# One order for every step of the attention stage: the transposes first, the projection matmuls in one run, VectorE's other work behind the maximum

## The chip, the cores and the metric

The kernel runs on one core of one Trainium2 chip. The metric is the time of one execution in device microseconds; shorter is better. TensorE is written PE, VectorE DVE, ScalarE ACT, GpSimd POOL, and SP is the queue that issues most transfers.

## What is computed

One encoder layer over 512 tokens of width 2048, in float32. An input projection gives queries, keys, values and gates for two groups of 16 heads; the group A heads use a dilated attention over all 512 keys with a bias table, the group B heads a neighbourhood attention on an 8 x 64 grid. Gated outputs go through an output projection and a layer norm.

```python
def reference(x, w_in, w_out, t5_bias, na_rpb, ln_gain, ln_bias):
    for layer in range(DEPTH):
        h = jnp.einsum('bsd,de->bse', x, w_in[layer])
        qa, ka, va, ga, qb, kb, vb, gb = jnp.split(h, splits, axis=-1)
        ya = _dilated_attention(heads(qa, N_HEADS_A), heads(ka, N_HEADS_A), heads(va, N_HEADS_A), t5_bias)
        yb = _neighbourhood_attention(heads(qb, N_HEADS_B), heads(kb, N_HEADS_B), heads(vb, N_HEADS_B), na_rpb[layer])
        ya = merge(ya) * jax.nn.silu(ga.astype(jnp.float32))
        yb = merge(yb) * jax.nn.silu(gb.astype(jnp.float32))
        out = jnp.einsum('bse,ed->bsd', jnp.concatenate([ya, yb], axis=-1), w_out[layer])
        x = _layer_norm(DEEPNORM_ALPHA * x + out, ln_gain[layer], ln_bias[layer])
    return x
```

## The kernel before

Every float32 operand of a large product is split into a high and a low part (two float32r tiles), and a product is three matmuls. Six gate columns come first, then six blocks of the input projection (queries, keys, values of both groups) by a Strassen scheme, then the attention stage (about 549 to 876 us of the profiled execution), then the rest of the output projection with the layer norm.

**The attention stage** is the loop `for n in range(136)` (L715). Step n takes one block of 128 queries of one head: head n // 4, block b = n % 4. Heads come in pairs of one group, A A B B A A ..., so a pair lasts 8 steps. The pieces of a step are:

- the scores (`scores`, L555): two matmuls into a PSUM bank `sc`, 512 columns wide in group A, 192 or 256 in group B; then on DVE the addition of the bias and the row extreme in one instruction (L525, called the maximum here), which frees the bank;
- the exponential (`exponent`, L529) on ACT;
- the turn of block n - 2 (`turn`, L581): four transposes in group A, two in group B, into a PSUM bank `pt`; then ACT copies the high part `th` (L593), and DVE subtracts it for the low part `tl` (L594), which frees the bank. `th` and `tl` of a head's four blocks lie in one tile each, "s0" and "s1", and there is one of each, so a new head's first `th` and `tl` must wait until the head before has been used;
- in the mixing steps (n % 4 == 2, from 6 to 130) the values of the head before (`values`, L599): eight matmuls into a bank of the same pool as the scores, first four that read `th`, then four that read `tl`; then ACT copies one half of the bank (`tmp`, L735), and DVE adds the other (`y`, L736), which frees the bank;
- the fillers: matmuls of the remaining gate columns (L464, while n is below about 63) and of the first half of the output projection (L658, after that), taken one at a time by `fill`. A step takes 8, 10, 8 or 1 of them up to n = 63, then 7, 8, 7 or 1 (1 in a mixing step).

Each filler weight is loaded, copied high on ACT (`wh`, L449) one step later and subtracted on DVE (`wl`, L450) two steps after its load was prepared, by a list of tasks per step (`later`), which `close` runs at the step's end. Other such tasks on DVE: the gate products (L633, L641, L643), the reciprocal of the denominators (L747), the gate's second half (L470), and the eviction of odd output banks (L664). After the fillers of each step with n % 8 == 1, `share` (L616) turns the pair's reciprocals into the other kind of row: one transpose into a bank of the turn's pool (two banks), a copy on ACT (L623), two transfers on POOL.

PE, ACT, DVE and SP run the stage in the order in which the code states it (`manual_schedule`, L708); POOL's order is the planner's. Semaphores follow from the tiles and banks.

Of the kernel before, what the change touches and what calls it, by code (L numbers as in the profile page):

```python
# [9 lines left out]
AF = mybir.ActivationFunctionType  # L10
ALU = mybir.AluOpType
# [59 lines left out]
def hybrid_layer(tc, xT, xn, w_in, w_early, w_gate, w_out, t5x, brow, rpb, cmask, eye, gain, lbias, out):  # L71
    nc = tc.nc
    from contextlib import ExitStack
    with ExitStack() as ctx:
# [8 lines left out]
        def f(ap):  # L83
            return ap.bitcast(F32)
# [9 lines left out]
        def slot(tag, dtype=F32, name=None):  # L94
            return arena.tile([128, sizes[tag[0]]], dtype, name=name or tag, tag=tag)

        class Ring:
# [3 lines left out]
            def next(self, name, dtype=F32):  # L101
                tag = self.tags[self.n % len(self.tags)]
                self.n += 1
                return slot(tag, dtype, name)

        def bank(pool, name):
            tag = {id(pacc): "acc", id(pss): "sc", id(pst): "pt"}[id(pool)]
            return pool.tile([128, 512], F32, name=name, tag=tag)
# [321 lines left out]
        step, tasks = [-PROLOGUE], {}  # L430
# [3 lines left out]
        def later(k, fn, dve=False):  # L434


            tasks.setdefault(step[0] + k, []).append((fn, dve))

        def prepare():

            while stream and len(raws) < 4:
                raws.append(raw_ring.next("wraw"))
                nc.sync.dma_start(raws[-1], stream.pop(0))
            if not raws:
                return
            raw = raws.pop(0)
            h, l = halves.next("wh", F32R), halves.next("wl", F32R)
            ready.append((h, l))
            later(1, lambda: nc.scalar.activation(h, raw, AF.Copy))  # L449
            later(2, lambda: nc.vector.tensor_tensor(l, raw, f(h), ALU.subtract), True)  # L450
# [59 lines left out]
        def load_sg(i):  # L510
            sgs[i] = sg_ring.next("sg")
            nc.sync.dma_start(sgs[i], sg_d[i])

        def softmax(sc, bias, n, grp, i, col, to=0, p=None):

            s = s_ring.next("s")
            p = p_ring.next("p") if p is None else p
            mn = small.tile([128, 1], F32, name="mn", tag="mn")
            if col == 0:
                dens[i] = small.tile([128, 8], F32, name="den", tag="den")  # L520
            den = dens[i][:, col:col + 1]
            flat = (s[:, :n], sc[:, :n])
            if grp == 1:
                flat = (t.rearrange("p (r c) -> p r c", r=8) for t in flat)
            nc.vector.tensor_tensor_reduce(*flat, bias, 1.0, 3e38, ALU.add, ALU.min, mn)  # L525
            order, c = "p (r b c) -> p b r c", 8 if grp else 16

            def exponent():
                nc.scalar.activation(p[:, to:to + n].rearrange("p (b r c) -> p b r c", r=8, c=c),  # L529
                                     s[:, :n].rearrange(order, r=8, c=c), AF.Exp, bias=mn, scale=-1.0, accum_out=den)  # L530
            return p, exponent

        COLS = ((0, 24), (8, 32), (24, 32), (40, 24))
        loaded, vs, biases, probs, turned, dens, sgs, yt, rcs = {}, {}, {}, {}, {}, {}, {}, {}, {}

        def head(h):

            g, j = ORDER[h // 2]
            return g, h // 2, h % 2, 2 * j + h % 2
# [15 lines left out]
        def scores(n):  # L555

            h, b = divmod(n, 4)
            g, i, a, _ = head(h)
            qt, ql, kt = loaded[i]
            cols = slice(128 * b, 128 * b + 128)  # L560
            sc = bank(pss, "sc")
            o, ko = sc, kt[:, a]
            if g:
                rows = "p (r w) -> p r w"
                c0, w = COLS[b]
                o = sc[:, :8 * w].rearrange(rows, r=8)
                ko = ko.rearrange(rows, r=8)[:, :, c0:c0 + w]
            nc.tensor.matmul(o, qt[:, a, cols], ko, start=True, stop=False)  # L568
            nc.tensor.matmul(o, ql[:, a, cols], ko, start=False, stop=True)  # L569
            if g == 0:  # L570
                p, exponent = softmax(sc, biases[h][:, 48 - 16 * b:560 - 16 * b], 512, 0, i, 4 * a + b)
                probs[n] = p, 4
                return exponent
            at = BIAS[(0, 1, 1, 2)[b]][0]
            outer = {0: (64, outers[h % 2][0]), 3: (0, outers[h % 2][1])}
            p, exponent = softmax(sc, biases[h][:, at:at + 8 * w].rearrange(rows, r=8), 8 * w, 1, i, 4 * a + b,
                                  *outer.get(b, ()))
            probs[n] = p, 2
            return exponent

        def turn(n):  # L581
            h, b = divmod(n, 4)
            p, nch = probs.pop(n)
            if b == 0:
                turned[h] = slot("s0", F32R, "th"), slot("s1", F32R, "tl")
            pt = bank(pst, "pt").rearrange("p (k q) -> p k q", k=4)
            for k in range(nch):
                nc.tensor.transpose(pt[:, k], p[:, k * 128:k * 128 + 128], ident)  # L588
            if head(h)[0] == 0:
                th, tl = (t.rearrange("p (k q) -> p k q", k=4)[:, :, 128 * b:128 * b + 128] for t in turned[h])  # L590
            else:
                th, tl = (t[:, 256 * b:256 * b + 256].rearrange("p (k q) -> p k q", k=2) for t in turned[h])
            nc.scalar.activation(th, pt[:, :nch], AF.Copy)  # L593
            nc.vector.tensor_tensor(tl, pt[:, :nch], f(th), ALU.subtract)  # L594

        near = ((0, 0, 256, 128), (2, 256, 512, 640), (1, 128, 384, 384), (3, 0, 512, 0))
        full = tuple((k, 0, 512, 512 * k) for k in range(4))
# [93 lines left out]
        def fill(n):  # L691
            for _ in range(n):
                next(filler, None)

        def close():

            for fn, dve in tasks.pop(step[0], ()):
                if dve and 5 <= step[0] < 128 and step[0] % 4 == 1:
                    held.append(fn)
                else:  # L700
                    fn()
            step[0] += 1
# [5 lines left out]
        with tc.manual_schedule(engines=engines):  # L708
            prepare()
            for _ in range(3):  # L710
                close()
            while step[0] < 0:
                fill(7)
                close()
            for n in range(136):  # L715
                b, i = n % 4, n // 8
                mixing = n % 4 == 2 and 6 <= n <= 130
                amount = (8, 8, 1, 8) if n < 64 else (7, 7, 1, 7)
                amount = amount[b] + (2 if n < 64 and b == 0 else 1 if b == 0 else 0)
                if b == 0 and n < 124:  # L720
                    load_bias(n // 4 + 1)
                if n % 8 == 0 and n < 120:
                    load_kq(i + 1)
                if n % 8 == 4 and n < 128:
                    if n < 120:
                        load_v(i + 1)
                    load_sg(i)
                exponent = scores(n) if n < 128 else None
                while held:
                    held.pop(0)()  # L730
                if mixing:
                    if exponent:
                        exponent()
                    mine, theirs, y, t = values(n // 4 - 1)
                    nc.scalar.activation(t, theirs, AF.Copy)  # L735
                    nc.vector.tensor_tensor(y, mine, t, ALU.add)  # L736
                    fill(amount)
                else:
                    fill(amount // 2)
                if 2 <= n < 130:  # L740
                    turn(n - 2)
                if not mixing:
                    if exponent:
                        exponent()
                    fill(amount - amount // 2)
                if n >= 8 and n % 8 == 0:
                    later(0, lambda i=i: nc.vector.reciprocal(dens[i - 1], dens[i - 1]), True)  # L747
                if n >= 8 and n % 8 == 1:
                    share(i - 1)
                if n >= 8 and n % 8 == 4:  # L750
                    later(0, lambda i=i: gate(i - 1), True)
                if n >= 8 and n % 8 == 7:
                    gated(i - 1)
                close()
            while tasks:
                close()
            fill(400)
            while tasks:
                close()
# [134 lines left out]
        for dc in (2, 3):  # L894
            for u in range(4, 8):
                raw = out_ring.next("wraw")
                nc.sync.dma_start(raw[:, :1024], w_out[8 * dc + u])
                i = 2 * (u - 4)
# [80 lines left out]
```

## Time and profile before

| | |
|---|---|
| median of 3 executions | 982.05 us (982.03 to 982.08) |
| the profiled execution's own time | 981.69 us |
| its span, first to last instruction | 979.9 us |
| PE busy | 969.0 us (99% of the span) |
| DVE busy | 757.6 us (77%) |
| ACT busy | 488.5 us (50%) |
| share of PE on the chain that ended last | 97% |

Busy times count an instruction from its start to its end. On PE, DVE and ACT instructions overlap a little, so the pace of an engine in a run of instructions is read from start to start, not from the durations. A wait is shown behind the instruction that waited, with what released it.

### The profile page before, as it was taken

Reading aid. Unit: us, or ns where it says so; the run is one execution under the profiler, and the core shown is the slowest. Engines: PE = TensorE matmul, PEld = TensorE weight load, DVE = VectorE, ACT = ScalarE, POOL = GpSimd, SP = SyncE. Lnnn points to the kernel's source line nnn. Section 1 sums busy time; section 2 is a strip of 40 time slices with the busy share of each in tenths; the row PEclk is TensorE's granted clock in tenths of the full one; section 3 lists DMA queues with packets and bytes.
Section 4 is the critical chain, followed back from the end, with each engine's and each line's share of the span. In section 5 each row is a group of like instructions: output and inputs, shape, how many; then the busy total and the mean of one; then the engine's idle time right before and its main releaser. Section 6 shows DMA issues by size and latency. Waiting matters only on the chain.

```text
span 979.9 us, 16071 instructions
## 1 busy us (share of the span) xinstructions
PE 969.0 (99%) x5851; PEld 855.5 (87%) x5851; DVE 757.6 (77%) x1152; ACT 488.5 (50%) x839; POOL 202.9 (21%) x327
## 2 busy tenths in 40 slices
PE   9999999999999999999999999999999999999996
PEld 7889999999888999999888888888888888888885
DVE  7958779778888887977988466677676767777877
ACT  7534344344444434435454356675666766673300
POOL 1003656744753620000000001010011000100021
PEclk9999999999999999999999999999999999999998
DMA  9833697699388559239544967777778778778212
GB/s 341 291 117 69 187 304 242 183 258 242 118 236 268 164 155 293 72 104 262 126 128 127 322 183 216 204 226 227 192 227 221 194 238 200 212 225 301 86 75 98
DMA packets 118015, 194.30 MB, mean 198 GB/s; under 512 B 48351, under 2 KB 67551, under 8 KB 117936
## 3 DMA queue, kind: packets, MB, share of 16 engines
q1 hardware_dynamic: 105104, 169.15, 57.6%
q0 software_dynamic: 12256, 23.47, 8.7%
q8 instruction: 46, 0.75, 0.3%
q10 hardware_dynamic: 576, 0.66, 0.2%
q14 instruction: 33, 0.27, 0.1%
HBM read 148.68 MB, written 44.50 MB: 197 GB/s over the span
## 4 chain that ended last, share of the span: by engine, by line
PE 97%; ACT 1%; DVE 1%; issue 0%; POOL 0%; DVEq 0%; ACTq 0%; POOLq 0%
PE acc L658 14%; PE acc L464 11%; PE acc L369 11%; PE acc L367 11%; PE acc L368 11%; PE acc L360 5%; PE acc L361 5%; PE acc L362 5%; PE pv L610 4%; PE pt L588 4%; PE acc L267 2%; PE acc L268 2%; PE acc L269 2%; PE sc L569 2%; PE sc L568 2%; PE sc L658 1%
## 5 line engine op out<-in xcount | busy, mean ns | idle before, releaser
L87 ACT ACTIVATE wh<-braw 128x1024 fp32r<-128x1024 f32 x168 | 178.3, 1061 | 243.5 <-PE acc L368 166.1
L88 DVE TENSOR_TENSOR wl<-braw,wh 128x1024 fp32r<-128x1024 f32 x168 | 206.2, 1229 | 76.5 <-ACT wh L87 76.4
L367 PE MATMUL acc<-xk,wh 128*128 128x256 f32 x512 | 143.6, 282 | 1.1 <-ACT wh L87 1.1
L368 PE MATMUL acc<-xk,wh 128*128 128x256 f32 x512 | 143.5, 282 | 0.0
L369 PE MATMUL acc<-xk,wl 128*128 128x256 f32 x512 | 141.1, 282 | 0.0
L375 DVE TENSOR_TENSOR braw<-braw 128x1024 f32<-128x1024 f32 x96 | 117.3, 1236 | 1.1
L594 DVE TENSOR_TENSOR tl<-pt,th 128x256 fp32r<-128x256 f32 (+1 forms) x128 | 71.0, 555 | 48.0 <-ACT th L593 46.8
L658 PE MATMUL acc<-wh,yk 128*128 128x512 f32 x320 | 108.1, 401 | 0.0
L367 PE MATMUL acc<-op,wh 128*128 128x256 f32 x384 | 107.4, 282 | 0.0
L368 PE MATMUL acc<-op,wh 128*128 128x256 f32 x384 | 107.4, 282 | 0.0
L369 PE MATMUL acc<-op,wl 128*128 128x256 f32 x384 | 105.2, 283 | 0.0
L367 PEld LDWEIGHTS acc<-xk,wh 128*128 128x128 f32 x512 | 97.2, 190 | 1.6 <-ACT wh L87 1.5
L368 PEld LDWEIGHTS acc<-xk,wh 128*128 128x128 f32 x512 | 97.2, 190 | 0.1
L369 PEld LDWEIGHTS acc<-xk,wl 128*128 128x128 f32 x512 | 95.8, 190 | 0.0
L593 ACT ACTIVATE th<-pt 128x256 fp32r<-128x256 f32 (+1 forms) x128 | 62.3, 489 | 64.8 <-PE pt L588 62.8
L464 PE MATMUL acc<-xk,wh 128*128 128x512 f32 x320 | 90.8, 402 | 0.0
L525 DVE CUSTOM_DVE_ANT_0 s<-sc,biases 128x512 f32<-128x512 f32 (+2 forms) x128 | 68.1, 532 | 17.9 <-PE sc L569 17.3
L529 ACT ACTIVATE p<-s,mn 128x512 f32<-128x512 f32 (+1 forms) x96 | 62.2, 647 | 25.8 <-DVE mn L525 25.5
L369 PEld LDWEIGHTS acc<-op,wl 128*128 128x128 f32 x384 | 71.5, 190 | 1.7 <-DVE wl L88 1.7
L367 PEld LDWEIGHTS acc<-op,wh 128*128 128x128 f32 x384 | 73.0, 190 | 0.0
L368 PEld LDWEIGHTS acc<-op,wh 128*128 128x128 f32 x384 | 73.0, 190 | 0.0
L658 PEld LDWEIGHTS acc<-wh,yk 128*128 128x128 f32 x320 | 58.5, 189 | 8.8
(183 smaller groups left out, 2039.3 us busy)
## 6 DMA issues: line engine op xcount, KB each, us to landing
braw<-in_w_in SPq DMA_DIRECT2D x96, 512.0 KB
wraw<-in_w_out SPq DMA_DIRECT2D x32, 512.0 KB
wraw<-in_w_gate SPq DMA_DIRECT2D x20, 512.0 KB
k_d<-kst SPq DMA_DIRECT2D x64, 128.0 KB
q_d<-kst SPq DMA_DIRECT2D x64, 128.0 KB
v_d<-vst SPq DMA_DIRECT2D x32, 256.0 KB
q<-q_d SPq DMA_DIRECT2D x32, 256.0 KB
k<-k_d SPq DMA_DIRECT2D x16, 512.0 KB
```

Source lines behind the costliest of these rows:

```text
L87: nc.scalar.activation(hi, raw, AF.Copy)
L88: nc.vector.tensor_tensor(lo, raw, f(hi), ALU.subtract)
L367: nc.tensor.matmul(o, h[:, c], ah, start=k == 0 and n == 0, stop=False)
L368: nc.tensor.matmul(o, h[:, c], al, start=False, stop=False)
L369: nc.tensor.matmul(o, l[:, c], ah, start=False, stop=k == 7 and n == 1)
L375: nc.vector.tensor_tensor(dst[u], dst[u], other[u], ALU.add)
L464: nc.tensor.matmul(acc, w[:, k * 128:k * 128 + 128], X[8 * u + k][:, s], start=u == 0 and n == 0 and k == 0, stop=u == 1 and n == 2 and k ...
L525: nc.vector.tensor_tensor_reduce(*flat, bias, 1.0, 3e38, ALU.add, ALU.min, mn)
L529: nc.scalar.activation(p[:, to:to + n].rearrange("p (b r c) -> p b r c", r=8, c=c), s[:, :n].rearrange(order, r=8, c=c), AF.Exp, bias=mn, ...
L593: nc.scalar.activation(th, pt[:, :nch], AF.Copy)
L594: nc.vector.tensor_tensor(tl, pt[:, :nch], f(th), ALU.subtract)
L658: nc.tensor.matmul(acc[:, part], yk[k][:, s, c], w[:, wk], start=first and kk == 0 and n == 0, stop=last and kk == 1 and n == 2)
```

## The change

No instruction is added or taken away; four engines get another order inside the step.

- On PE the turn moves from the middle of the step (in mixing steps from its end) to its head, ahead of the scores, and all fillers follow in one run.
- On ACT and DVE the copy `th` and the subtraction `tl` become `copy_turned`, placed after the maximum and after held tasks, before the exponential. In a mixing step they now stand ahead of the copy and the addition of the values.
- DVE tasks of every step from 5 to 127 are held until the next step's maximum has been issued; before, only those of steps with n % 4 == 1. The reciprocal is no longer such a task and runs at its own step's end.

```diff
@@ turn(n) @@
             for k in range(nch):
                 nc.tensor.transpose(pt[:, k], p[:, k * 128:k * 128 + 128], ident)
+            turns[n] = pt[:, :nch]
+
+        def copy_turned(n):
+
+            h, b = divmod(n, 4)
+            pt = turns.pop(n)
             if head(h)[0] == 0:
                 th, tl = (t.rearrange("p (k q) -> p k q", k=4)[:, :, 128 * b:128 * b + 128] for t in turned[h])
             else:
                 th, tl = (t[:, 256 * b:256 * b + 256].rearrange("p (k q) -> p k q", k=2) for t in turned[h])
-            nc.scalar.activation(th, pt[:, :nch], AF.Copy)
-            nc.vector.tensor_tensor(tl, pt[:, :nch], f(th), ALU.subtract)
+            nc.scalar.activation(th, pt, AF.Copy)
+            nc.vector.tensor_tensor(tl, pt, f(th), ALU.subtract)
@@ close() @@
-                if dve and 5 <= step[0] < 128 and step[0] % 4 == 1:
+                if dve and 5 <= step[0] < 128:
                     held.append(fn)
@@ the loop over n @@
+                if 2 <= n < 130:
+                    turn(n - 2)
                 exponent = scores(n) if n < 128 else None
                 while held:
                     held.pop(0)()
+                if 2 <= n < 130:
+                    copy_turned(n - 2)
+                if exponent:
+                    exponent()
                 if mixing:
-                    if exponent:
-                        exponent()
                     mine, theirs, y, t = values(n // 4 - 1)
                     nc.scalar.activation(t, theirs, AF.Copy)
                     nc.vector.tensor_tensor(y, mine, t, ALU.add)
-                    fill(amount)
-                else:
-                    fill(amount // 2)
-                if 2 <= n < 130:
-                    turn(n - 2)
-                if not mixing:
-                    if exponent:
-                        exponent()
-                    fill(amount - amount // 2)
+                fill(amount)
                 if n >= 8 and n % 8 == 0:
-                    later(0, lambda i=i: nc.vector.reciprocal(dens[i - 1], dens[i - 1]), True)
+                    later(0, lambda i=i: nc.vector.reciprocal(dens[i - 1], dens[i - 1]))
```

## Rows read from the trace of the kernel before

**Rows 1.** The page's first part: busy time of each engine, its share of the span, number of instructions.

```profile
PE 969.0 (99%) x5851; PEld 855.5 (87%) x5851; DVE 757.6 (77%) x1152; ACT 488.5 (50%) x839; POOL 202.9 (21%) x327
```

**Rows 2.** Busy time by stretch, over the attention stage (548.9 to 876 us): the stretch and its length, then each engine's busy time, the granted TensorE clock (PEclk, 1.00 is full speed), the share of the DMA engines, GB/s; last the sum over the five stretches of the stage.

```profile
740.00:865.00 125.00, 124.84 (x679) 103.87 (x678) 92.31 (x217) 86.03 (x203) 9.44 (x18) 1.00 0.78 214
...
sum 327.10, PE 326.94 PEld 272.18 DVE 229.14 ACT 210.95 POOL 29.41; mean PE 65.39 PEld 54.44 DVE 45.83 ACT 42.19 POOL 5.88
```

**Rows 3.** Waits of the weight loads (PEld) in the stage: total us, times, longest.

```profile
PEld pv L610 <- ACT th L593: 0.7, 2, 0.4
```

**Rows 4.** The chain that ended last, before the first step: start, length, a run of 49 fillers with nothing between them.

```profile
548.90 11.11 PE acc L464 x49
```

**Rows 5.** PE in order of time around the mixing step 22, in a pair of group A: start, length, instructions merged when equal. L568 and L569 are scores, L610 values, L588 the turn, L464 fillers.

```profile
616.27 0.39 PE L568 MATMUL sc<-k,q 128*128 128x512 f32 x1
616.50 0.39 PE L569 MATMUL sc<-k,ql 128*128 128x512 f32 x1
616.73 1.09 PE L610 MATMUL pv<-th,vv 128*128 128x512 f32 x4
...
618.56 0.39 PE L464 MATMUL acc<-xk,wh 128*128 128x512 f32 x1
618.79 0.60 PE L588 MATMUL pt<-ident,p 128*128 128x128 f32 x4
619.14 0.48 PE L568 MATMUL sc<-k,q 128*128 128x512 f32 x1
...
619.69 1.09 PE L464 MATMUL acc<-xk,wh 128*128 128x512 f32 x4
620.62 0.60 PE L588 MATMUL pt<-ident,p 128*128 128x128 f32 x4
620.98 0.48 PE L464 MATMUL acc<-xk,wh 128*128 128x512 f32 x1
621.29 0.86 PE L464 MATMUL acc<-xk,wl 128*128 128x512 f32 x3
```

**Rows 6.** The same view around the mixing step 26, in a pair of group B, with its narrow scores.

```profile
629.93 0.38 PE L588 MATMUL pt<-ident,biases 128*128 128x128 f32 x2
630.07 0.34 PE L568 MATMUL sc<-k,q 128*128 128x192 f32 x1
...
630.35 0.64 PE L464 MATMUL acc<-xk,wh 128*128 128x512 f32 x2
...
631.29 0.38 PE L588 MATMUL pt<-ident,p 128*128 128x128 f32 x2
631.43 1.18 PE L464 MATMUL acc<-xk,wl 128*128 128x512 f32 x4
632.45 0.25 PE L568 MATMUL sc<-k,q 128*128 128x192 f32 x1
...
632.64 0.65 PE L464 MATMUL acc<-xk,wl 128*128 128x512 f32 x2
```

**Rows 7.** DVE in order of time, in two stretches; in brackets the idle time before an instruction and what ended it.

```profile
616.93 0.69 DVE L525 CUSTOM_DVE_ANT_0 s<-sc,biases 128x512 f32<-128x512 f32 x1
...
619.38 0.68 DVE L736 TENSOR_TENSOR y<-pv,tmp 64x512 f32<-64x512 f32 x1 [1.16 <-ACT tmp L735]
620.12 0.69 DVE L594 TENSOR_TENSOR tl<-pt,th 128x512 fp32r<-128x512 f32 x1
620.72 1.22 DVE L450 TENSOR_TENSOR wl<-wraw,wh 128x1024 fp32r<-128x1024 f32 x1
621.86 0.68 DVE L525 CUSTOM_DVE_ANT_0 s<-sc,biases 128x512 f32<-128x512 f32 x1
...
622.46 0.69 DVE L594 TENSOR_TENSOR tl<-pt,th 128x512 fp32r<-128x512 f32 x1
623.07 0.68 DVE L641 TENSOR_TENSOR y<-y,rc 128x512 f32<-128x512 f32 x1
623.67 0.35 DVE L525 CUSTOM_DVE_ANT_0 s<-sc,biases 128x192 f32<-128x192 f32 x1
623.94 0.09 DVE L525 DVE_READ_ACCUMULATOR2_ANT mn<- 128x1 f32 x1
...
681.92 0.41 DVE L594 TENSOR_TENSOR tl<-pt,th 128x256 fp32r<-128x256 f32 x1
682.25 0.34 DVE L525 CUSTOM_DVE_ANT_0 s<-sc,biases 128x192 f32<-128x192 f32 x1
```

**Rows 8.** ACT in order of time in step 22: the exponential, then the copy of the values' half, which waited for the last value matmul.

```profile
617.72 0.72 ACT L529 ACTIVATE p<-s,mn 128x512 f32<-128x512 f32 x1
...
618.76 0.59 ACT L735 ACTIVATE tmp<-pv 64x512 f32<-64x512 f32 x1 [0.22 <-PE pv L610]
```

**Rows 9.** PE and ACT in order of time from the `share` of step 17 (L619, copied by L623) to the values of step 18, whose head is of group B.

```profile
605.36 0.27 PE L619 MATMUL pt<-ident,den 128*8 128x128 f32 x1
...
605.38 0.48 PE L568 MATMUL sc<-k,q 128*128 128x512 f32 x1
...
605.66 0.27 ACT L623 ACTIVATE tmp<-pt 8x128 f32<-8x128 f32 x1
...
605.93 0.63 PE L610 MATMUL pv<-th,vv 128*128 128x256 f32 x4
...
606.88 0.40 PE L464 MATMUL acc<-xk,wh 128*128 128x512 f32 x1
```

More of the change, by code (lines that the diff above doesn't have):

```diff
@@ L533, in hybrid_layer @@
         COLS = ((0, 24), (8, 32), (24, 32), (40, 24))
-        loaded, vs, biases, probs, turned, dens, sgs, yt, rcs = {}, {}, {}, {}, {}, {}, {}, {}, {}
+        loaded, vs, biases, probs, turned, dens, sgs, yt, rcs, turns = {}, {}, {}, {}, {}, {}, {}, {}, {}, {}
         def head(h):
```

## The prediction, written before the changed kernel was timed

> **What bounds the kernel now.** I read the page's first part, then the busy time by stretch, the waits and the order of time on each engine. PE is busy for 969.0 of the 979.9 us span [rows 1]. The change touches only the attention stage, and there PE is busy for 326.94 of 327.10 us at a granted clock of 1.00 (2.4 GHz, the upper of its two levels) [rows 2]. The only waits listed for it are two of a weight load, 0.7 us together, mostly hidden behind the matmul still running [rows 3]. So in this stage PE waits for nobody: the stage is as long as its matmuls, start to start. No order on ACT or DVE can shorten it; a new order can only make a matmul cheaper by its neighbours, or make PE wait where it does not now.
>
> **The order on PE, costed.** The fillers run at 11.11 / 49 = 0.227 us before the first step [rows 4], and at (620.62 - 619.69) / 4 = 0.2325 us inside the stage [rows 5]; that mean is used below for a plain filler.
>
> - Now: a turn of four transposes between fillers takes 620.98 - 620.62 = 0.36 us, and the filler behind it 621.29 - 620.98 = 0.31, that is 0.08 above a plain one. A pair of wide scores between fillers takes 616.73 - 616.27 = 0.46. Together 0.36 + 0.08 + 0.46 = 0.90 us [rows 5].
> - After the change: turn, scores, filler. The trace has this order already, where a mixing step ends and the next begins: from the turn at 618.79 to the filler at 619.69, 0.90 us [rows 5]. The 0.08 falls on the first score instead of the filler.
> - Group B: two transposes 631.43 - 631.29 = 0.14, the four fillers behind them 632.45 - 631.43 = 1.02, 0.09 above four plain ones, scores 632.64 - 632.45 = 0.19, together 0.42. In the new order, 630.35 - 629.93 = 0.42 [rows 6].
>
> So the new order on PE costs nothing and brings nothing. A small term remains. The 0.2325 against 0.227 is an excess of about 0.005 us a matmul that shows where turns are near [rows 4, 5]. The stage has about 815 fillers (864 less the 49 ahead of it). If one long run loses the excess, the gain is at most 815 x 0.0055 = 4.5 us; if the more even spacing of turns spreads it, since today turn and mixing step leave one run of up to 15 matmuls without a turn, the loss is below 1 us. The run without turns shows no excess [rows 4] and there are as many turns as before; I take +0.3 us, nearer the second end.
>
> **ACT and DVE: what becomes late.** The number of instructions is the same, so only waits count. Paces from start to start [rows 7]: wide maximum 0.60 us (621.86 to 622.46), narrow 0.27 (I take 0.35 at 256 columns, in proportion), `tl` 0.60 or 0.33 (681.92 to 682.25), `wl` 1.14 (620.72 to 621.86), other 512-wide work 0.60. A maximum starts 616.93 - 616.50 = 0.43 us after the second score starts [rows 5, 7].
>
> *Mixing steps.* The new head's `th` waits for the four value matmuls that read the old `th`, since there is one such tile; `tl` waits for the other four. Behind `th` on ACT stand the exponential (0.72) and the values' copy (0.59) [rows 8]; behind `tl` on DVE stands `y`. In a step of two B heads: values start 0.46 us into it, the first half ends near 1.1, `th` to 1.4, exponential to 1.9, copy to 2.5, `y` to 3.1. Before, the copy came straight behind the values, so `y` comes some 0.6 us later. Who waits: the values' bank serves the scores two steps on, at 1.64 + 2.04 + 0.14 = 3.8 us (step lengths from the pieces above: 0.46 + 0.95 + 0.23, the values from [rows 9]; then 0.42 + 7 x 0.2325). That leaves 0.7 us. With A heads all is longer, the values 1.83 us [rows 5], and about 1 us is left. Both can be passed only if `th` waited for much more than I assume; even the whole of the values (0.4 us more in B, 0.9 in A) leaves a little. Cost: nothing.
>
> *Filler weights.* `wl` comes a step later, behind the next maximum. In the gate columns the low part is used after 16 matmuls, two steps on. In the output products it is the third matmul. Tightest is the first, prepared around step 61 and subtracted in step 63: counted from step 62, `y` ends at 3.1, the maximum 3.4, `wl` 4.6; PE wants it at 3.9 (step 64) + 0.14 + 0.55 + 0.23 = 4.8. It just fits; the later ones use it later in the step. Cost: nothing.
>
> *Values behind held work.* In steps with n % 8 == 5 the gate product (0.60) now stands ahead of `tl`, which the next step's values read in their second half. `tl` ends some 3 us into step n, and values want it 1.4 us after step n ends. Cost: nothing.
>
> *The turn at the head of the step.* Its bank is normally that of the turn two steps before. But in steps with n % 8 == 1 `share` takes a bank of this pool too. The turn in the next step (15 of them, n = 10 to 122) then needs the bank whose `tl` belongs to the step just ended, or the one `share` used. Before, that turn stood at the end of a mixing step, 1.4 to 2.5 us later. This is where the cover is gone: behind a waiting turn stand the step's scores, values and fillers on PE, so the wait counts in full. In the gate half, with 8 and 10 fillers, about 0.4 us is left. In the output half it is tight. The worst kind is step 82, with an output bank to evict in step 81. From the start of step 78: `y` to 3.1; step 79's maximum to 3.4, `wl` 4.5, `tl` 4.9; step 80's maximum 5.5, a gate product 6.1, `tl` 6.4, reciprocal 6.6; step 81's maximum starts at 7.1 (its scores set it) and ends 7.7, eviction 8.3, `tl` 8.7. Steps 78 to 81 last 1.64 + 2.04 + 2.54 + 2.34 = 8.56 us, so PE waits about 0.25 us with the signal. Step 98 is the same, and step 114 follows a step with three held pieces (`wl`, eviction, gate product), some 0.5 us. The other five of this half come out between 0.3 us early and 0.1 late. Sum: 0.25 + 0.25 + 0.5 + about 0.1 = 1.1 us. Its lower end is nothing, when the planner hands out a bank already free.
>
> SP issues the same transfers at the head of the same steps; a bias load waits for the last maximum of the head before, which comes up to 0.7 us later and is wanted four steps (10 us) on. POOL sends the gate rows one step later and they are read pairs later. Cost of both: nothing.
>
> Sum: +0.3 + 1.1 = +1.4 us at the most likely, with the last term more often smaller than larger; I take +1.0. On the profiled execution that is 981.69 + 1.0 = 982.7, and on the median 983.0 us. A measurement of this kernel can tell about 0.2%, 2 us, so I call it no change.
>
> **A rule on DVE's pace.** Rows 7 show the next DVE instruction starting 0.07 to 0.09 us before the one ahead ends (`tl` at 620.12 lasts 0.69, the next starts at 620.72) [rows 7]. The Trainium skill (VectorE: DVE Perf Modes, The DRAIN you can't avoid) says that the next operation does not start until the pipeline is empty. By that rule each of the nine steps of the chain above would cost 0.08 more, and the turn's wait in step 82 would be 0.9 us instead of 0.25, an estimate. The row decides, but its direction is that of the second rival.
>
> **The rivals.**
>
> - *The share's bank (slower).* If the turn in step 8i + 2 is given the bank of `share`, it waits for ACT's copy: 605.66 + 0.27 - 605.36 = 0.57 us after the transpose began, against 0.02 for the next matmul [rows 9]. 15 x 0.55 = 8.3, with the 0.3 above: 990.6 us. For it: the pool has two banks. Against it: the other bank comes free earlier in most steps. It decides where the planner picks by its own times. Chance 0.10.
> - *DVE's held work later than worked out (slower).* If the chain of held work ends 0.4 us later than I have it, the eight turns behind a `share` in the output half wait, 0.25 to 0.9 us each, some 4.5 us with a filler weight or two: 986.9 us. For it: in those steps DVE's work and the step's length differ by less than 0.3 us. Against it: over this half DVE is busy for 92.31 of 125 us even by durations that overlap [rows 2], so a late step is made good in the next. It decides from a lag of about 0.3 us in steps with n % 8 == 1. Chance 0.22.
> - *Runs at the undisturbed pace (faster).* One run of 7 to 10 fillers goes at 0.227: 982.05 - 4.5 = 977.6 us. For it: [rows 4]. Against it: the excess follows the turn, and the turns stay. Chance 0.08.
>
> **How the numbers follow.** No change that can be told, 0.60, with its own range 981.0 to 984.0 (part of the excess lost, to all bank waits at their upper end); the second rival 0.22, up to 988; the first 0.10; faster 0.08. The predicted time is that of the first. The range runs from 981.0 to 988.0 and leaves out the share's bank and the undisturbed runs, 0.18 together. Faster 0.08, same 0.60, slower 0.22 + 0.10 = 0.32.
>
> **What would show it.** In the changed trace the turn, the scores and the first filler should take 0.90 us in group A and 0.42 in group B, PE should still be busy for all but about 1 us of the stage, and `y` should start later behind the values than now, where it starts 619.38 - 618.56 = 0.82 us after the filler that follows them [rows 5, 7]. Waits should stand at the turn (L588) in steps 82, 98 and 114, with the release by `tl` (L594) and none at fillers, scores or values. Waits of half a microsecond at each turn behind a `share`, released by L623, would be the first rival; many waits at L588 released by L594 in the output half, the second; fillers at 0.227 us between turns, the third. The prediction is wrong if a bank or the single `th` tile holds PE in every head, or if the price of a transpose depends on what follows it in a way that the mixing steps of now do not show.

## The result and the profile after

The changed kernel takes 983.45 us (median of 21 executions, 982.93 to 984.37) against 982.08 us (981.57 to 983.03) before: a ratio of 1.0014, 95% interval 1.0008 to 1.0020. That is 1.4 us more, less than the 2 us that the prediction counts as no change, and 0.45 us above the predicted 983.0. The interval leaves out 1, so with this many executions it is a small loss and not nothing. Its profiled execution took 984.37 us, the longest of the 21, so its trace shows somewhat more loss than the usual execution has; the trace of seven below, of a kernel with 15 more additions, stands nearer to the median.

The first part of the page and the busy time of the engines in two stretches of the attention stage, of the changed kernel (the sum is over 549 to 865 us):

```profile
PE 969.2 (99%) x5851; PEld 856.0 (87%) x5851; DVE 757.4 (77%) x1152; ACT 492.3 (50%) x839; POOL 199.2 (20%) x327
...
655.00:740.00 85.00, 84.92 (x456) 70.67 (x455) 60.90 (x139) 56.05 (x131) 9.19 (x18) 1.00 0.72 209
740.00:865.00 125.00, 122.95 (x667) 102.27 (x666) 91.73 (x212) 85.44 (x199) 9.44 (x18) 1.00 0.80 213
sum 316.00, PE 313.87 PEld 261.31 DVE 219.36 ACT 204.99 POOL 27.85; mean PE 104.62 PEld 87.10 DVE 73.12 ACT 68.33 POOL 9.28
```

Over the whole execution PE's work is what it was (969.2 us here, 969.0 in [rows 1]). In the stage PE is now without work for 2 us where it was without work for 0.2 [rows 2], and nearly all of that lies in the output half, 740 to 865 us. The granted clock is 1.00 in both, so the clock has no part in it.

The waits in the stage (what waited, for what: us in total, times, longest):

```profile
ACT th L599 <- PE pv L616: 30.2, 26, 2.1
...
PE pt L588 <- DVE tl L600: 2.0, 3, 1.1
...
DVE y L647 <- DMA rc<-rc_d: 1.4, 1, 1.4
```

PE waits only at the turn (L588), for `tl`, three times listed: in steps 82, 98 and 114, the ones that the prediction named. ACT's copy `th` waits in 26 steps for the value matmuls, 30 us in all, and none of it shows as a wait of PE. `y` starts later behind the values, as forecast: in step 22 it is 1.22 us after the filler that follows them instead of 0.82. The third line, a product on DVE that waits for a transfer, is the line that the prediction did not have.

PE in order of time at two steps: the turn, the scores and the first filler, in a pair of group A and in one of group B.

```profile
760.69 0.38 PE L588 MATMUL pt<-ident,p 128*128 128x128 f32 x2
760.82 0.34 PE L568 MATMUL sc<-k,q 128*128 128x192 f32 x1
...
761.11 0.41 PE L664 MATMUL acc<-wl,yk 128*128 128x512 f32 x1
...
776.28 0.60 PE L588 MATMUL pt<-ident,p 128*128 128x128 f32 x4
776.63 0.47 PE L568 MATMUL sc<-k,q 128*128 128x512 f32 x1
...
777.17 0.39 PE L664 MATMUL acc<-wh,yk 128*128 128x512 f32 x1
...
767.59 0.27 PE L625 MATMUL pt<-ident,den 128*8 128x128 f32 x1
768.91 0.63 PE L588 MATMUL pt<-ident,p 128*128 128x128 f32 x4 [1.05 <-DVE tl L600]
...
844.97 0.27 PE L625 MATMUL pt<-ident,den 128*8 128x128 f32 x1
846.08 0.63 PE L588 MATMUL pt<-ident,p 128*128 128x128 f32 x4 [0.83 <-DVE tl L600]
```

From the turn to the first filler it is 777.17 - 776.28 = 0.89 us in group A and 761.11 - 760.69 = 0.42 in group B, as [rows 5] and [rows 6] have it: the new order is as dear as the old. The last four rows are steps 81 to 82 and 113 to 114. A `share` (L625) that nothing hinders is followed by the turn 0.11 us later; here the turn comes 1.32 and 1.11 us later, that is 1.2 and 1.0 us of waiting. The same reading over all fifteen such places, from `share` to turn less 0.11, gives 0.05 at step 10, 0.25 at 66, 1.2 at 82, 0.33 at 98, 0.06 at 106, 1.0 at 114, 0.06 at 122 and nothing at the other eight: 3.0 us.

**Two waits that went away.** The values of one head before the change, and the same eight matmuls after it, PE in order of time:

```profile
805.57 1.01 PE L610 MATMUL pv<-th,vv 128*128 128x256 f32 x4
806.42 0.64 PE L610 MATMUL pv<-tl,vv 128*128 128x256 f32 x4
```

```profile
808.02 0.64 PE L616 MATMUL pv<-th,vv 128*128 128x256 f32 x4
808.50 0.52 PE L616 MATMUL pv<-tl,vv 128*128 128x256 f32 x3
```

The first four took 806.42 - 805.57 = 0.85 us before and take 808.50 - 808.02 = 0.48 now. The other of the two weight loads in [rows 3] cost 0.31 in the same way (0.79 against 0.48). Both are gone: 0.68 us gained. The same two are gone in each of the kernels below too, also in two and three, which have one half of the change each.

**The account.** From the start of the stage's first filler to the start of its last value matmul, the profiled execution took 336.00 us before and 337.90 after; the last value matmul now stands two fillers earlier in the order, so 0.46 is added: 2.36 us more. Waits at the turn +3.0, waits in the values -0.7, and some 0.05 us is left for PE's new order.

### The profile page after: what moved, and what is told of

It is laid out like the page before. It is cut to its first block, busy times and chain, and to the rows that moved or that the text cites. A ratio compares the mean times of both kernels' runs of the same rounds, so it can differ in the third digit from the quotient of the medians.

```text
span 982.6 us, 16082 instructions
## 1 busy us (share of the span) xinstructions
PE 969.2 (99%) x5851; PEld 856.0 (87%) x5851; DVE 757.4 (77%) x1152; ACT 492.3 (50%) x839; POOL 199.2 (20%) x327
## 4 chain that ended last, share of the span: by engine, by line
PE 87%; issue 6%; DMA 3%; DVE 2%; POOL 1%; ACT 0%; DVEq 0%; POOLq 0%
PE acc L664 12%; PE acc L369 11%; PE acc L367 11%; PE acc L368 11%; PE acc L464 8%; PE acc L360 5%; PE acc L361 5%; PE acc L362 5%; PE pv L616 3%; PE pt L588 3%; PE acc L267 2%; PE acc L268 2%; PE acc L269 2%; DMA rc_d<-tmp 2%; PE sc L569 2%
## 5 line engine op out<-in xcount | busy, mean ns | idle before, releaser
L664 PE MATMUL acc<-wh,yk 128*128 128x512 f32 x320 | 103.6, 393 | 0.0
L599 ACT ACTIVATE th<-pt 128x256 fp32r<-128x256 f32 (+1 forms) x128 | 62.4, 487 | 53.3 <-PE pv L616 30.2
L464 PE MATMUL acc<-xk,wh 128*128 128x512 f32 x320 | 83.4, 392 | 0.0
```

What stands on the lines that cost most here:

```text
L464: nc.tensor.matmul(acc, w[:, k * 128:k * 128 + 128], X[8 * u + k][:, s], start=u == 0 and n == 0 and k == 0, stop=u == 1 and n == 2 and k ...
L599: nc.scalar.activation(th, pt, AF.Copy)
L664: nc.tensor.matmul(acc[:, part], yk[k][:, s, c], w[:, wk], start=first and kk == 0 and n == 0, stop=last and kk == 1 and n == 2)
```

## The experiments

All times are medians of five rounds; before took 982.07 us beside them. The numbers are those of the runs' labels, in which four and five do not occur.

**One: the turns out of the way of `share`'s bank.** `share` takes its bank from the scores' pool.

```diff
-            turn8 = bank(pst, "pt")[0:8, 0:128]
+            turn8 = bank(pss, "sc")[0:8, 0:128]
```

> The changed kernel, with one edit: the share's transpose takes a bank of the scores' pool instead of the turn's. Theory (the bank): the 1.4 us that the change cost are some 2.9 us of waits of the turn behind a share, less about 1 us that the longer filler runs give back. With the bank gone from the turn's pool no turn waits more than 0.1 us, and the time is 983.45 - 2.9 = 980.6 us, ratio to the kernel before 0.9985 (0.998 to 0.999). Rival (the order itself costs, by the neighbours of the transposes): the time stays at 983.4, ratio 1.0014. A third way: the wait moves to the scores that follow a share, since their pool has two banks too, and the time lies between.

986.30 us (985.94 to 986.66), ratio 1.0041 (1.0029 to 1.0054). No turn waits any more, but the kernel is slower than the changed one. PE's waits at the values, ACT and PE in order of time at one of them:

```profile
PE pv L616 <- DVE mn L525: 1.4, 2, 0.8
...
PE pv L616 <- ACT tmp L629: 1.3, 2, 1.1
```

```profile
769.29 1.04 ACT L449 ACTIVATE wh<-wraw 128x1024 fp32r<-128x1024 f32 x1
...
770.24 0.25 ACT L629 ACTIVATE tmp<-sc 8x128 f32<-8x128 f32 x1
770.54 0.74 PE L616 MATMUL pv<-th,vv 128*128 128x256 f32 x4 [1.07 <-ACT tmp L629]
```

The scores' pool has two banks as well, and the values and the scores take them in turn. `share`'s bank comes free only with its copy (L629), which stands on ACT behind a filler's `wh`, and the values wait for it. Where the values get the bank of the scores just made, they wait for its maximum (the first line). The two lines do not list all of it: start to start, the stage's scores and values take 104.5 us here and 99.0 in the changed kernel, so 5.5 us are lost there where 3.0 are gained at the turn. The run shows that the waits hang on the turn's pool, and that a bank borrowed elsewhere moves them; it does not tell what the kernel would be without them.

**Two and three: the two parts of the change apart.** The second kernel is the changed one with DVE's tasks held as before, so it has PE's new order and the copies' new place on ACT and DVE; the third is the kernel before with only DVE's tasks held in every step.

```diff
 two, on the changed kernel:
-                if dve and 5 <= step[0] < 128:
+                if dve and 5 <= step[0] < 128 and step[0] % 4 == 1:
...
-                    later(0, lambda i=i: nc.vector.reciprocal(dens[i - 1], dens[i - 1]))
+                    later(0, lambda i=i: nc.vector.reciprocal(dens[i - 1], dens[i - 1]), True)
 three, on the kernel before:
-                if dve and 5 <= step[0] < 128 and step[0] % 4 == 1:
+                if dve and 5 <= step[0] < 128:
...
-                    later(0, lambda i=i: nc.vector.reciprocal(dens[i - 1], dens[i - 1]), True)
+                    later(0, lambda i=i: nc.vector.reciprocal(dens[i - 1], dens[i - 1]))
```

> The changed kernel with the holding of DVE tasks put back: only those of steps with n % 4 == 1 are held, the reciprocal among them; PE's order and the place of the copies stay changed. Theory (held work makes the bank late): without evictions, gate products and filler weights between maximum and tl, most waits at the turn go; 0.3 us or less remain, and the time is near 980.9 us, ratio 0.9988. Rival (the order itself): 983.4, ratio 1.0014. If the waits stay but the holding is not their cause: also 983.4, with L588 still waiting for L600.

> The kernel before with the other half alone: DVE tasks of every step held until the next maximum, the reciprocal at its own step's end; the turn stays in the middle of the step. Theory (the bank at the head of the step): the turn comes 1.4 us or more later than the bank is free, PE does not wait, and the time is that of before, 982.1 us, ratio 1.000 (0.9995 to 1.0005). Rival (held work costs by itself, by low parts and evictions that come late): 983 us or more, ratio 1.001.

Two: 985.26 us (984.93 to 985.82), ratio 1.0032 (1.0020 to 1.0043). It was expected to be the faster one and is the slower one: my theory that the held tasks make the turn wait falls. Its waits at the turn, worked out as above, sum to 4.3 us instead of 3.0. Its DVE before step 114, with the one row of ACT that bears on it:

```profile
841.03 1.22 DVE L450 TENSOR_TENSOR wl<-wraw,wh 128x1024 fp32r<-128x1024 f32 x1
842.16 0.68 DVE L670 COPY z<-acc 128x512 f32<-128x512 f32 x1
842.76 0.68 DVE L647 TENSOR_TENSOR y<-y,rc 128x512 f32<-128x512 f32 x1
843.36 0.68 DVE L525 CUSTOM_DVE_ANT_0 s<-sc,biases 128x512 f32<-128x512 f32 x1
...
844.09 0.72 ACT L529 ACTIVATE p<-s,mn 128x512 f32<-128x512 f32 x1 [2.24 <-DVE mn L525]
...
846.21 0.42 DVE L600 TENSOR_TENSOR tl<-pt,th 128x256 fp32r<-128x256 f32 x1 [1.15 <-ACT th L599]
```

and that of the changed kernel in the same steps, down to the `tl` for which the turn waits:

```profile
841.01 0.69 DVE L525 CUSTOM_DVE_ANT_0 s<-sc,biases 128x512 f32<-128x512 f32 x1
841.62 1.22 DVE L450 TENSOR_TENSOR wl<-wraw,wh 128x1024 fp32r<-128x1024 f32 x1
842.76 0.68 DVE L670 COPY z<-acc 128x512 f32<-128x512 f32 x1
843.36 0.69 DVE L647 TENSOR_TENSOR y<-y,rc 128x512 f32<-128x512 f32 x1
844.41 0.64 DVE L525 CUSTOM_DVE_ANT_0 s<-sc,biases 128x512 f32<-128x512 f32 x1
845.50 0.42 DVE L600 TENSOR_TENSOR tl<-pt,th 128x256 fp32r<-128x256 f32 x1 [0.45 <-ACT th L599]
```

The work is the same; held back, the maximum of step 112 comes at 841.01 instead of 843.36, so that step's exponential can run 2.3 us earlier (841.74 instead of 844.09). Without holding, the exponential waits on ACT 2.24 us for the maximum, the `th` behind it is late, and `tl` starts at 846.21, 0.71 us later than above, while `share` is only 0.24 later.

Three: 981.49 us (981.19 to 981.75), ratio 0.9993 (0.9984 to 1.0002), not to be told from before. PE has no gap there (the output half of the stage):

```profile
740.00:865.00 125.00, 125.00 (x681) 104.33 (x680) 93.58 (x219) 86.59 (x206) 9.43 (x18) 1.00 0.77 214
```

So the new order on PE with the copies' new place costs 985.26 - 982.07 = 3.2 us without the holding, the holding alone nothing that can be told (the medians differ by 0.6 us, and the interval reaches from a gain of 1.6 us to a loss of 0.2), and both together 1.4: the held tasks take back part of what the turn's new place costs. No run moves the turn on PE without moving its copies, so the two are not told apart.

**Six and seven: the same work ahead of `tl` and behind it.** An addition of no use to the output, 0.6 us on DVE, in every step n % 8 == 1: the steps that end with a `share`.

```diff
 six:
                 while held:
                     held.pop(0)()
+                if 9 <= n < 128 and n % 8 == 1:
+                    nc.vector.tensor_tensor(tmp, biases[n // 4][:, :512], biases[n // 4][:, :512], ALU.add)
                 if 2 <= n < 130:
                     copy_turned(n - 2)
 seven: the same two lines behind copy_turned
```

> The changed kernel with a 512-wide addition of 0.6 us more on DVE, of no use to the output, ahead of the copies (th, tl) in the 15 steps with a share (n % 8 == 1). Theory (the bank): each turn behind a share in the output half (8 of them) waits up to 0.6 us more, each in the gate half (7) 0.2 us more after its margin of 0.4: 983.45 + 4 to 6 = about 988 us, ratio 1.006, with the waits at L588. Rival (the order itself, DVE off the path): DVE has room, 983.5, ratio 1.0014.

> As the run with 0.6 us more on DVE ahead of the copies in the steps with a share, with the same 15 additions behind the copies instead. The run with them ahead took 987.16 us. Theory (tl of the step with the share is what the next turn waits for, so only work ahead of it counts): 983.5 to 984.3 us, ratio 1.0015 to 1.0025. Rival (DVE's load as a whole sets the pace in these steps): 986 to 987 us, as with the additions ahead.

Six: 987.16 us (986.92 to 987.29), ratio 1.0050 (1.0037 to 1.0062), 3.7 above the changed kernel, a little less than the 4 to 6 expected; its waits at the turn sum to 5.4 us, 4.8 of it in the output half. Seven: 983.52 us (982.99 to 984.34), ratio 1.0017 (1.0008 to 1.0025), the changed kernel's time. So the same 15 additions cost 3.6 us ahead of `tl` and nothing behind it: in these steps not DVE's amount of work counts but that `tl` of the step with the `share` ends in time. PE's waits at the turn in six:

```profile
PE pt L588 <- DVE tl L600: 2.6, 4, 0.9
PE pt L588 <- ACT tmp L629: 1.1, 3, 0.4
```

The second line is the first rival of the prediction: at three turns (steps 10, 66 and 106) PE waited for `share`'s copy on ACT, so the planner had given the turn `share`'s own bank. By what it chooses is not shown; in the changed kernel itself no such wait is listed.

Seven is also a second look at the turns of the changed kernel, since its additions change nothing ahead of a `tl`: another kernel, but one of the same time, and its profiled execution (983.64 us) lies near the changed kernel's median. PE and DVE around step 82 there:

```profile
767.85 0.27 PE L625 MATMUL pt<-ident,den 128*8 128x128 f32 x1
768.21 0.63 PE L588 MATMUL pt<-ident,p 128*128 128x128 f32 x4
```

```profile
764.92 0.68 DVE L647 TENSOR_TENSOR y<-y,rc 128x512 f32<-128x512 f32 x1
765.52 0.41 DVE L600 TENSOR_TENSOR tl<-pt,th 128x256 fp32r<-128x256 f32 x1
```

The turn comes 0.36 us behind `share` instead of 1.32: a wait of 0.25 instead of 1.2. The difference stands in the changed kernel's DVE and POOL at that place:

```profile
764.06 0.67 DVE L525 CUSTOM_DVE_ANT_0 s<-sc,biases 128x512 f32<-128x512 f32 x1
...
766.13 0.69 DVE L647 TENSOR_TENSOR y<-y,rc 128x512 f32<-128x512 f32 x1 [1.39 <-DMA rc<-rc_d]
766.74 0.42 DVE L600 TENSOR_TENSOR tl<-pt,th 128x256 fp32r<-128x256 f32 x1
...
767.75 0.69 DVE L670 COPY z<-acc 128x512 f32<-128x512 f32 x1
768.35 0.42 DVE L600 TENSOR_TENSOR tl<-pt,th 128x256 fp32r<-128x256 f32 x1
```

```profile
759.57 1.05 POOL L632 DMA_DIRECT2D rc<-rc_d  x2 [7.93 <-DMA rc_d<-tmp]
```

and POOL in seven:

```profile
759.41 1.05 POOL L632 DMA_DIRECT2D rc<-rc_d  x2 [7.52 <-DMA rc_d<-tmp]
```

The product `y` x `rc`, a held task of step 79, now stands on DVE ahead of a `tl`, and it waits 1.39 us for `rc`. In seven's trace it does not wait, though POOL issued the transfer nearly as late there, after 7.52 us of waiting for the one before it. The difference lies for the most part in the transfer itself: from issue to landing `rc` took 5.8 to 6.0 us in the changed kernel's trace and 4.5 to 4.7 in seven's. At the other turns the two traces agree within 0.01 us, so the waits sum to 2.0 us in seven and its stage is 336.92 + 0.46 - 336.00 = 1.4 us longer than before, which is the difference of the medians.

**Eight: the turn behind a `share` put back where it was.** In the fifteen steps n = 10, 18, ... the turn and its copies come after the fillers, all else as in the changed kernel.

```diff
+                late = n >= 10 and n % 8 == 2
-                if 2 <= n < 130:
+                if 2 <= n < 130 and not late:
                     turn(n - 2)
...
-                if 2 <= n < 130:
+                if 2 <= n < 130 and not late:
                     copy_turned(n - 2)
...
                 fill(amount)
+                if late and n < 130:
+                    turn(n - 2)
+                    copy_turned(n - 2)
```

> The changed kernel, but in the 15 steps behind a share (n % 8 == 2) the turn and its two copies stand where they stood before, at the end of the step behind the fillers. In all other steps the change stays. Theory (the price of the change is the turn's wait for a bank behind a share, and nothing else of PE's order costs): no wait at the turn, and the time is 983.45 less the 2.9 us of waits, more what the waits had hidden: 980.7 to 981.6 us, ratio 0.9987 to 0.9996. Rival (the order of all 128 steps costs a little each): 15 of 128 steps put back bring back 0.2 us of the 1.4, 983.2 us, ratio 1.0012. A wait moved elsewhere, as with the share's bank in the scores' pool, would show at the values.

981.21 us (980.82 to 983.41), ratio 0.9996 (0.9987 to 1.0005): 2.2 us below the changed kernel, and not to be told from before. PE has no gap left in the output half, and no turn waits for its bank:

```profile
740.00:865.00 125.00, 125.00 (x680) 104.64 (x679) 93.83 (x218) 87.76 (x205) 9.95 (x19) 1.00 0.80 216
```

With these fifteen turns and their copies moved the whole loss of the change is gone. With all other turns at the head and the fillers in one run, the stage is 334.62 + 0.46 - 336.00 = -0.9 us against before, of which 0.7 is the two waits at the values: PE's new order itself brings 0.2 us, which is nothing.

**Nine: `share` inside the run of fillers**, two fillers into its step, instead of behind the run.

```diff
+                sharing = n >= 8 and n % 8 == 1
+                if sharing:
+                    fill(2)
+                    share(i - 1)()
+                    amount -= 2
```

(The diff is shortened: `share` returns `send` instead of giving it to the step's end, the call behind the run is gone, and the lines shown stand ahead of the exponential.)

> The changed kernel, but the share's transpose stands behind the second filler of its step instead of behind the last, and its copy on ACT stands ahead of the exponential. The share still takes a bank of the turn's pool. Theory (the bank): the share's own bank is free some 0.5 us before the step ends, so the next turn finds a bank if it gets that one: 981 us, ratio 0.999, no wait at the turn. If the planner keeps giving it the other bank, the waits stay at L588 for L600, and the time is 983 to 984, or worse, since the exponential now waits for the share. Rival (order): 983.4.

982.30 us (981.91 to 984.18), ratio 1.0005 (0.9996 to 1.0014), against an expected 981. No turn waits, but `share` itself does, some 1.2 us in all over four steps. The longest, PE in order of time:

```profile
843.23 0.27 PE L625 MATMUL pt<-ident,den 128*8 128x128 f32 x1 [0.66 <-DVE den L754]
844.50 0.60 PE L588 MATMUL pt<-ident,p 128*128 128x128 f32 x4
```

The reciprocal that it reads (L754) runs on DVE at the end of the step before, and `share` now wants it some 1.2 us (five fillers) earlier.

**Ten: the product two steps later**, with what hangs on it.

```diff
-            later(0, lambda: nc.vector.tensor_tensor(y, y, rcs[i], ALU.mult), True)
-            later(1, lambda: nc.scalar.activation(t[:, 0], y, AF.Copy, scale=0.5))
-            later(2, lambda: nc.vector.scalar_tensor_tensor(...), True)
+            later(2, lambda: nc.vector.tensor_tensor(y, y, rcs[i], ALU.mult), True)
+            later(3, lambda: nc.scalar.activation(t[:, 0], y, AF.Copy, scale=0.5))
+            later(4, lambda: nc.vector.scalar_tensor_tensor(...), True)
```

> The changed kernel with the three pieces of the gated output (the product with the reciprocals, its high copy, its low part) two steps later each. In the changed kernel's trace the product of step 80 waited 1.39 us for its transfer, with tl and the next maximum behind it, and the turn of step 82 waited 1.05 us. Theory (that transfer makes step 82's wait, and held work those of steps 98 and 114): the wait of step 82 falls to 0.3 us or less, those of 98 and 114 fall by up to 0.6 us each since the product stands no longer in the step before the share, and the time is 983.45 - 0.8 to 2 = 981.5 to 982.6 us, ratio 0.9994 to 1.0005. Rival (the transfer is a symptom): 983.4.

982.50 us (982.03 to 983.74), ratio 1.0005 (0.9997 to 1.0014), 0.95 us below the changed kernel. The waits at the turn sum to 0.8 us (0.25 each at steps 66, 82 and 98, 0.05 at step 10); at step 114 there is none (PE in order of time):

```profile
844.22 0.27 PE L625 MATMUL pt<-ident,den 128*8 128x128 f32 x1
844.33 0.60 PE L588 MATMUL pt<-ident,p 128*128 128x128 f32 x4
```

In exchange a filler's weight load waits for the product's low part, which costs 0.2 us. So the product, with the copy that hangs on it, is what made step 114 late, and ACT in the changed kernel shows the way it went:

```profile
844.08 0.64 ACT L648 ACTIVATE yk<-y 128x512 fp32r<-128x512 f32 x1 [1.52 <-DVE y L647]
844.62 0.58 ACT L672 ACTIVATE z<-acc 128x512 f32<-128x512 f32 x1
845.10 0.38 ACT L599 ACTIVATE th<-pt 128x256 fp32r<-128x256 f32 x1
```

ACT's copy of the product waits 1.52 us for DVE, an eviction follows, and `th` stands behind both; the `tl` at 845.50 above had been idle 0.45 us for that `th`.

## Why the prediction was right, and where it was not

**What bounds the stage** held but for the 0.7 us below. PE sets the pace in both kernels, and it lost only at the turn; the kernels in which the turn does not wait and nothing waits in its place (three and eight) stand beside before. As busy time can hide a wait, these two were read start to start as well: no matmul of their stages comes more than 0.11 us later than is usual for its kind and place.

**The order on PE**: 0.90 and 0.42 us were read off the mixing steps, and 0.89 and 0.42 came out. For the term of +0.3 us the account leaves 0.05 us in the changed kernel, -0.2 in eight. The third rival fell: in the runs between two turns the fillers of the changed kernel go at 0.231 us on average, at 0.240 directly behind the scores and at 0.227 only by the ninth.

**The two waits of rows 3** were called mostly hidden. They were not: they cost 0.68 of their 0.7 us, and the change took them away. That is a gain of 0.7 us which the sum did not have. The step that failed is reading "the matmul is still running" as cover; start to start, the four matmuls took 0.85 us where 0.48 is usual. With it falls the sentence that no order on ACT or DVE can shorten the stage: in three DVE's order alone removes both waits, and its stage is 0.3 us shorter (335.72 against 336.00).

**The turn behind `share`** is the right place and the right mechanism, released by `tl` as predicted, with no wait at fillers, scores or values. The term was mis-sized: 1.1 us predicted, 2.0 in seven's trace near the median, 3.0 in the changed kernel's own. By step: 0.25 predicted for 82 and 0.25 measured when `rc` is in time (in seven `share` starts 8.54 us after step 78 and `tl` ends after 8.75, where 8.56 and 8.7 were worked out); 0.25 against 0.33 at 98; 0.1 for the other five of the output half against 0.37 (0.25 of it at 66); none in the gate half against 0.05. The two large errors are these:

- Step 114, 0.5 against 1.0. The working followed DVE's queue alone. The wait came over ACT, where `th` is queued behind a copy that waits for the held product. The prediction named the three held pieces ahead of that `tl`, but not who on ACT waits for one of them. DVE's queue alone comes near the predicted 0.5: `tl` at 845.50 had been idle 0.45 for `th`, and without that the wait would be some 0.55, an estimate.
- Step 82, 0.25 against 1.2 in one trace. The working counted the gate product with its 0.6 us and not with a wait of its own. It waits for a transfer, and everything behind it on DVE, the `tl` among it, waits too. The prediction costed POOL's gate rows at nothing, had no term for the transfer of `rc`, and did not ask which instruction would stand on DVE and wait for one.

**The three terms** give 0.05 + 2.0 - 0.7 = 1.35 us near the median, against 0.3 + 1.1, taken as 1.0. That the total was right within half a microsecond is in part luck: a gain that was missed paid for most of a loss that was sized too small.

**The other items costed at nothing** held: the `th` in the mixing steps (30.2 us of waiting on ACT, none on PE), the filler weights (0.07 us, at the first low part in step 64, which the working called the tightest), SP.

**The rivals.** `Share`'s bank did not decide in the changed kernel, but six shows that it is real. DVE's held work late, 4.5 us, is what two shows in its number (4.3 us of waits), but with the sign of the cause reversed: that happens without holding, and holding lessens it. On the pace of DVE the rule weighed in the prediction (the Trainium skill, VectorE: DVE Perf Modes, The DRAIN you can't avoid) gave 0.9 us at step 82. The rows above show `tl` starting at 768.35 where the copy ahead of it ends at 767.75 + 0.69 = 768.44, and seven's turn waits 0.25. The same section goes on to say that an operation that is not held starts earlier, which the prediction left out and which is what these rows show.

**Left open**: whether eight is faster than before (0.9987 to 1.0005 holds both); how often `rc` comes late at step 82 (the product waits for it 1.39 us in the trace of the changed kernel, 1.34, 0.69 and 0.43 in those of one, two and eight, and not at all in those of six, seven and nine), and why; what the turn's new place costs on PE apart from that of its copies; and which of the turn's two banks the planner gives under which times.

## What to carry to other kernels

Where the engine that sets the end has no gaps, an instruction moved to the head of its step is priced by the buffer it takes: with two banks, one further user in the step before turns a wait that was two steps away into one on the step just ended. Follow the release of that buffer over every engine and queue it passes, and list what stands ahead of it, with what each of those pieces may itself wait for, transfers included. A task held back behind another is not only later itself: it lets the other through earlier, so try the two halves of a reordering apart before the loss is put down to either.

## What was not expected of the hardware

The small transfers behind `share` are long and vary from trace to trace by more than most of the waits at stake. 4 KB to memory (`rc_d<-tmp`) held POOL for 7.93 us in the changed kernel's trace and 7.52 in seven's; what is read back then took 5.8 to 6.0 us from issue to landing in the one and 4.5 to 4.7 in the other, and the product that reads it waited 1.39 us in the one and not at all in the other. Four transposes and the two wide scores cost PE the same in either order, 0.89 against 0.90 us.
